# The opening of a two-layer trunk with its column blocks dealt out anew and one narrow block for the gates, and another order of retention's items

## The chip, the cores and the metric

The kernel runs on one core of one Trainium2 chip. The metric is the time of the whole program on the device, in microseconds (us). Five engines matter in what follows: PE (TensorE, the matrix unit; PEld is its loading of the stationary operand), DVE (VectorE), ACT (ScalarE), POOL (GpSimd) and SP (SyncE, which here only issues transfers). Each works through its own list of instructions; between engines there are semaphores.

## The reference

A vector `c` is turned into a modulation vector, and a trunk of two layers works on `x` of 1024 positions by 1024 features. Layer 0 mixes with a gated delta rule (GDN), layer 1 with retention; a gated feed-forward part with a short causal convolution follows each.

```python
e = silu(c @ cond_w + cond_b)                      # 1024 x 1024
for i in range(2):
    sh1, sc1, g1, sh2, sc2, g2 = split(e @ ada_w[i] + ada_b[i], 6)   # 1024 x 6144
    y = mixers[i](x * (1.0 + sc1) + sh1)
    x = layer_norm(DN_ALPHA * x + (1.0 + g1) * y, ln_g[i, 0], ln_b[i, 0])
    y = conv_ffn(x * (1.0 + sc2) + sh2, ...)
    x = layer_norm(DN_ALPHA * x + (1.0 + g2) * y, ln_g[i, 1], ln_b[i, 1])

def gated_deltanet(h, w_in, ...):                  # 8 heads of 128, chunks of 64
    qkv, z, a, bt = split(h @ w_in, [3072, 4096, 4104])   # a and bt: 8 columns each
    qkv = silu(causal_dwconv(qkv, conv_w))         # 4 taps
    beta = sigmoid(bt);  g = -exp(a_log) * softplus(a + dt_bias)
    ...                                            # triangular solve and a scan over chunks

def retention(h, w_in, w_out):                     # 4 heads, 256 wide keys, 512 wide values
    q, k, v, gate = split(h @ w_in, [1024, 2048, 4096])
    q, k = rot(q), rot(k)                          # rotary positions
    ...                                            # decayed attention in chunks of 128
    o = standardize(o) * silu(gate)
    return o @ w_out
```

`a` and `bt` together are the 16 columns called the gates' columns of GDN here. Retention's `gate` (2048 columns) is something else.

## The kernel before, in words

All arrays are float32. A product that has to be exact is made of three matmuls in the fast float32 form: each operand is split into a high part (a rounding copy on ACT, line 89) and a low part (a subtraction on DVE, line 90), and PE adds up high by low, low by high and high by high (`mm3`, lines 107 to 112). A tile is 128 partitions wide; rows of x are handled in two halves of 512. A load of a weight block of 1024 x 128 is one transfer of 512 KB (`load_w`, line 102).

**Opening.** `cond_w` arrives in 8 pieces of 128 rows (line 182, two halves of 256 KB each). Of the 1024 output columns DVE takes 512, multiplying and adding piece by piece into `mva` (lines 184 and 186); PE takes the other four blocks of 128 columns, one accumulation bank each (`by_cols`, line 175). `col_sum` (line 170) then sums DVE's part over the partitions by four small matmuls with a vector of ones. With the bias and Silu this is `e` (line 203). The first quarter of the first layer's modulation (`mod_cols(0)`, lines 539 to 551) goes the same way, with 256 columns on DVE and two blocks on PE; quarters 1 to 3 are all DVE's, 512 columns each, with a column sum on PE (line 546). Their results are the scale and shift of features 2g and 2g+1 of h.

Four blocks of GDN's input weights are worked on meanwhile (`load_first`): block 0 is `wab`, the 16 gates' columns filled up with zeros to 128, blocks 1 to 3 belong to q, k and v. `x` is transposed on PE (`turn`, line 560, the copy at line 571). `first_k(half, f)` scales one feature block of 128 (line 577), splits it into `hT` (lines 89, 90) and adds its products into the accumulators: four for half 0, two for half 1. Between pairs of features stands one quarter of the modulation, so the opening has four stages. In the trace, line 110 is high by low, line 111 low by high, line 112 high by high. At the end the gates' columns are copied off (`ab`, line 634), transposed on PE (line 670) and worked into `g` and `beta` (lines 742, 743).

**Retention's input product.** The 3072 columns of q, k and gate are made with Strassen's scheme (`strassen`): for each item seven products (line 1179 in the trace) and sums on DVE and ACT. The list `mixed` says in which order the items come. A rope item applies the rotary positions with six DVE operations per half (lines 1672 to 1677), reading tiles with sines and cosines, and stores its halves to `qd` from ACT's queue (line 1679). A gate item applies Silu (line 1688) and stores to `gd` (line 1689). Both use the tiles called `pc`. After the last item the 2048 columns of v follow as an ordinary product (line 667), whose weights `ret_wv` are loaded at line 102 into the two-tile pool `wr`; half 1 of h comes back in pieces `xlo` (line 1705), turned at line 280. Meanwhile the residual is scaled by the layer norm's gain (`xg`, loads at lines 399 and 403, POOL at lines 409 and 410, stores at line 411), and q and k are read back (line 1843).

**What sets the order.** Within GDN's and retention's cores PE's order comes from a planner in the file; elsewhere the code's order is rearranged when the program is built, by a scheduler that times the engines by estimates. All loads and some stores are issued by SP in one order, and a load whose target is not yet free holds up every load behind it; the stores of `qd` and `gd` are issued by ACT. Tiles come from small pools (`wr` 2, `hTa` 8, `aux` 4, `auh` 8, `t2` 3), accumulators from 4 + 2 + 2 PSUM banks (`acc`, `mm`, `sc`).

## Time and profile before

| | us |
|---|---|
| median of three runs | 2954.41 (2944.8, 2956.14, 2954.41) |
| the profiled execution's own time | 2954.0 |
| its span, first to last instruction | 2952.2 |
| PE busy | 2822.2 (96%) |
| DVE busy | 2212.5 (75%) |
| ACT busy | 1316.4 (45%) |
| POOL busy | 494.4 (17%) |
| mean granted clock of TensorE | 0.982 |

PE's busy time is that of its records, whose ends are modelled; a chain of matmuls that starts one every 0.227 us counts as fully busy. The profile gives, for any stretch of time, the busy time of each engine with its number of instructions, the clock, the share of the transfer engines' time and their rate, and a timeline with what each instruction had waited for. Two stretches are of interest below: the opening, 0 to about 90 us, and the change from retention's items to its v product, about 1735 to 1770 us.

### The profile page before, as it was taken

The page shows a single profiled execution, that of the slowest core. Times are in us where ns is not written, and L with a number is a line of the kernel's source. Part 1 is how long each engine was busy: PE and PEld are TensorE (multiplying, and loading weights), DVE is VectorE, ACT ScalarE, POOL GpSimd, SP SyncE. Part 2 cuts the span into 40 slices and gives each one's busy share as a digit, 9 for nine tenths or more (in the row PEclk, how much of TensorE's full clock was granted, in tenths as well). Part 3 has the DMA queues.
Part 4 walks back from the last instruction along what each step waited for, and adds up shares of the span by engine and source line. Part 5 has one row for each costly group of instructions (what it writes and reads, how often), then busy time and mean ns, then how long its engine had stood idle before and what let it go on. Part 6 is the DMA issues. An engine that isn't in the chain of part 4 may idle for free.

```text
span 2952.2 us, 38981 instructions
## 1 busy us (share of the span) xinstructions
PE 2822.2 (96%) x13638; PEld 2306.3 (78%) x13638; DVE 2212.5 (75%) x3973; ACT 1316.4 (45%) x2413; POOL 494.4 (17%) x517
## 2 busy tenths in 40 slices
PE   8999898999999999998999999999999899999997
PEld 7787777887787888887878877777777788888886
DVE  5788787656688888958686665666779787777779
ACT  4745565444544444545333332221344544445543
POOL 0312221100013332000000012422202023331001
PEclk9999999999999999999999999999999999999999
DMA  7232222253255655855343364655673353334853
GB/s 277 86 108 68 83 79 80 83 166 138 93 178 173 213 187 191 300 156 176 130 140 121 115 217 154 210 170 164 186 242 125 106 168 128 136 129 161 293 182 114
DMA packets 248276, 459.40 MB, mean 156 GB/s; under 512 B 23632, under 2 KB 77136, under 8 KB 248080
## 3 DMA queue, kind: packets, MB, share of 16 engines
q1 hardware_dynamic: 215680, 405.27, 41.8%
q10 hardware_dynamic: 29760, 43.00, 4.0%
q0 software_dynamic: 2640, 8.65, 0.8%
q8 instruction: 107, 1.75, 0.3%
q14 instruction: 89, 0.73, 0.1%
HBM read 344.11 MB, written 112.72 MB: 155 GB/s over the span
## 4 chain that ended last, share of the span: by engine, by line
PE 73%; DVE 13%; DMA 6%; ACT 4%; issue 2%; POOL 1%; SPq 0%; POOLq 0%; ACTq 0%; DVEq 0%
PE acc L667 15%; PE acc L1179 9%; PE acc L110 5%; PE acc L111 5%; PE acc L112 5%; PE sc L1179 4%; PE sc L667 4%; PE acc L1454 3%; PE mm L667 3%; PE sc L111 2%; PE sc L112 2%; PE sc L110 2%; DVE o L1583 1%; PE mm L1454 1%; PE sc L1454 1%
## 5 line engine op out<-in xcount | busy, mean ns | idle before, releaser
L667 PE MATMUL acc<-hT,wh 128*128 128x512 f32 x960 | 300.2, 394 | 0.0
L1454 PE MATMUL acc<-bb,ab 128*128 128x512 f32 x984 | 236.7, 399 | 12.1 <-DVE bb L90 10.5
L1454 PEld LDWEIGHTS acc<-bb,ab 128*128 128x128 f32 x984 | 186.4, 191 | 56.1 <-DVE bb L90 15.5
L1179 PE MATMUL acc<-T,wb 128*128 128x512 f32 x840 | 203.2, 391 | 6.3 <-DVE wb L90 6.2
L667 PEld LDWEIGHTS acc<-hT,wh 128*128 128x128 f32 x960 | 182.3, 190 | 34.1
L89 ACT ACTIVATE ab<-ar 128x512 fp32r<-128x512 f32 x210 | 130.1, 626 | 166.5 <-PE mm L301 47.8
L667 PE MATMUL acc<-hT,wl 128*128 128x512 f32 x480 | 201.3, 419 | 0.0
L90 DVE TENSOR_TENSOR ab<-ar,ab 128x512 fp32r<-128x512 f32 x210 | 148.5, 713 | 65.2 <-ACT ab L89 65.2
L409 POOL TENSOR_TENSOR xg<-xg,gb 128x512 f32<-128x512 f32 x48 | 62.6, 1304 | 776.3 <-DMA xg<-xs 453.1
L1179 PEld LDWEIGHTS acc<-T,wb 128*128 128x128 f32 x840 | 156.7, 188 | 43.6 <-DVE wb L90 9.0
L90 DVE TENSOR_TENSOR wl<-wr,wh 128x1024 fp32r<-128x1024 f32 x95 | 119.8, 1262 | 88.3 <-ACT wh L89 88.1
L90 DVE TENSOR_TENSOR wb<-wr,wb 128x512 fp32r<-128x512 f32 x162 | 115.8, 720 | 71.5 <-ACT wb L89 71.4
L89 ACT ACTIVATE wh<-wr 128x1024 fp32r<-128x1024 f32 x95 | 100.7, 1061 | 146.4 <-PE acc L667 66.9
L90 DVE TENSOR_TENSOR wb<-mm,wb 128x512 fp32r<-128x512 f32 x216 | 145.8, 684 | 26.5 <-ACT wb L89 25.7
L1604 POOL TENSOR_TENSOR o<-o 128x512 f32<-128x512 f32 x80 | 111.7, 1405 | 287.6 <-ACT pc L1240 190.0
L1583 DVE SCALAR_TENSOR_TENSOR o<-g,vc,o 128x512 f32<-128x512 f32 (+2 forms) x176 | 154.7, 896 | 5.3 <-ACT o L1578 4.7
L89 ACT ACTIVATE wb<-mm 128x512 fp32r<-128x512 f32 x216 | 124.1, 595 | 59.8 <-DVE mm L1229 55.0
L1240 ACT ACTIVATE pc<-acc 128x512 f32<-128x512 f32 x143 | 84.8, 593 | 145.3 <-PE acc L1179 93.1
L89 ACT ACTIVATE wb<-wr 128x512 fp32r<-128x512 f32 x162 | 98.4, 627 | 104.5 <-DMA wr<-in_ffn_up 49.3
L667 PE MATMUL acc<-wh,hT 128*128 128x512 f32 x384 | 139.2, 425 | 2.9 <-DVE vv L90 1.7
L110 PE MATMUL acc<-T,wb 128*128 128x512 f32 x292 | 116.0, 397 | 9.4 <-DVE wb L90 9.4
L488 DVE SCALAR_TENSOR_TENSOR qkv<-raw,vc,qkv 128x512 f32<-128x512 f32 x144 | 111.7, 780 | 11.5 <-ACT qkv L486 10.7
(639 smaller groups left out, 7488.1 us busy)
## 6 DMA issues: line engine op xcount, KB each, us to landing
wr<-in_ffn_up SPq DMA_DIRECT2D x92, 512.0 KB, 4.3
mvw<-in_ada_w SPq DMA_DIRECT2D x80, 512.0 KB, 4.5
ad<-o SPq DMA_DIRECT2D x154, 256.0 KB, 3.1
ar<-ad SPq DMA_DIRECT2D x154, 256.0 KB, 3.8
Br<-in_ffn_down SPq DMA_DIRECT2D x88, 256.0 KB, 3.4
wr<-in_ret_wv SPq DMA_DIRECT2D x32, 512.0 KB, 4.1
ar<-od SPq DMA_DIRECT2D x56, 256.0 KB, 5.3
xs<-xt ACTq DMA_DIRECT2D x24, 512.0 KB, 3.8
```

What stands on the lines that cost most here:

```text
L89: act.activation(dst_h, src, AF.Copy)
L90: eng.tensor_tensor(dst_l, src, dst_h, ALU.subtract)
L110: mm(acc, wl[:, k], hl[0], start=first, stop=False)
L111: mm(acc, wh[:, k], hl[1], start=False, stop=False)
L112: mm(acc, wh[:, k], hl[0], start=False, stop=last)
L488: dve.scalar_tensor_tensor(oh, raw[:, 3 - j:515 - j], w[:, 3 - j:4 - j], oh, ALU.mult, ALU.add)
L667: pq(pe.matmul(out, lhsT, rhs, start=start, stop=stop), cost)
L1179: return pe.matmul(*a, skip_group_check=True, **kw)
L1240: act.activation(t, X, AF.Copy)
L1454: return pe.matmul(*args, skip_group_check=True, **kw)
L1583: dve.scalar_tensor_tensor(tv, gv[:, c0 - j:c1 - j], w[:, 2 - j:3 - j], tv, ALU.mult, ALU.add)
L1604: (dve if fp == 0 else pool).tensor_tensor(o[d], o[x], o[y], op)
```

## The change

1. **cond_w.** DVE takes five of the eight column blocks of `cond_w` (640 columns), PE three. The sum over the partitions covers five blocks.
2. **First quarter of the modulation.** DVE takes three blocks (384 columns), PE one.
3. **The gates' columns.** `wab` is laid out as 128 rows of 8 x 32 values, the 16 columns twice for each of the 8 feature blocks (128 KB instead of 512 KB). On the chip the second 16 of each 32 are replaced by their low part. A product with the gates' columns then takes two matmuls with 32 output rows (the high and low weight columns against `hT` high, and against `hT` low) instead of three with 128. The low part's rows are added after the transposes in `gates()`, by a copy and an addition per half; the copies and transposes cover 32 partitions instead of 128. A matmul with 32 stationary columns is in PE's form of 128 x 32 tiles, not 128 x 128.
4. **First stage.** The loads of the four weight blocks are issued together, and the splits, the turns and the products of features 0 and 1 are written block by block.
5. **Retention's items.** After two gate items the order was r r g r g r g r r g r g r g (r a rope item, g a gate item); it is now r r g r g r r g r g r r g g.

```diff
-    def col_sum(a, tile=None):
-        pt = (tile or mm_tile)()
-        for j in range(4 * len(a)):
-            pe.matmul(pt[:, j:j + 1], a[j // 4][:, j % 4 * P:j % 4 * P + P], ones[:, 0:1], start=True, stop=True)
+    def col_sum(a, n, tile):
+        pt = tile()
+        for j in range(n):
+            pe.matmul(pt[:, j:j + 1], a[:, j * P:(j + 1) * P], ones[:, 0:1], start=True, stop=True)
         return pt
 
     def by_cols(banks, w, v, k):
         for j, bank in enumerate(banks):
             pe.matmul(bank[:, 0:1], w[:, j * P:(j + 1) * P], v[:, k:k + 1], start=(k == 0), stop=(k == KT - 1))
 
-    a0 = tl("t2", [P, HALF], name="mva")
-    cbank = acc4()
+    NV = 5
+    a0 = tl("wr", [P, NV * P], name="mva")
+    cbank = [acc_tile() for _ in range(KT - NV)]
     for k in range(KT):
-        w = two("hTa", F32, "mvw")
+        w = tl("hTa", [P, D], name="mvw")
         for hf in range(2):
-            sp.dma_start(w[hf], A["cond_w"][k * P:(k + 1) * P, hs(hf)])
+            sp.dma_start(w[:, hs(hf)], A["cond_w"][k * P:(k + 1) * P, hs(hf)])
+        wv = w[:, 0:NV * P]
         if k == 0:
-            dve.tensor_scalar(a0, w[0], cT[:, 0:1], None, ALU.mult)
+            dve.tensor_scalar(a0, wv, cT[:, 0:1], None, ALU.mult)
         else:
-            dve.scalar_tensor_tensor(a0, w[0], cT[:, k:k + 1], a0, ALU.mult, ALU.add)
-        by_cols(cbank, w[1], cT, k)
+            dve.scalar_tensor_tensor(a0, wv, cT[:, k:k + 1], a0, ALU.mult, ALU.add)
+        by_cols(cbank, w[:, NV * P:], cT, k)
...
-    pt = col_sum([a0])
+    pt = col_sum(a0, NV, mm_tile)
...
+    raw1 = []
+    AB = 4 * GH
+
     def load_first(n):
         ti = first[n]
-        src = A["gdn_wab"] if ti is None else A["gdn_wqkv"][ti]
-        ws.append(load_w(src, ("wh", "wl") if n < 2 else ("aux", "aux"), "hTa"))
+        raw1.append(tl("hTa", [P, KT * AB if ti is None else D], name="wr"))
+        sp.dma_start(raw1[n], A["gdn_wab"] if ti is None else A["gdn_wqkv"][ti])
+
+    def split_first(n):
+        if first[n] is None:
+            w = tl("wh", [P, KT * AB], F32R, name="wab")
+            act.activation(w, raw1[n], AF.Copy)
+            wv, rv = [t.rearrange("p (k n) -> p k n", n=AB) for t in (w, raw1[n])]
+            dve.tensor_tensor(wv[:, :, AB // 2:], rv[:, :, AB // 2:], wv[:, :, AB // 2:], ALU.subtract)
+            ws.append(wv)
+            return
+        tags = ("wh", "wl") if n == 1 else ("aux", "aux")
+        w = [tl(tags[0], [P, D], F32R, name="wh"), tl(tags[1], [P, D], F32R, name="wl")]
+        split(w[0], w[1], raw1[n])
+        ws.append((kn(w[0]), kn(w[1])))
...
-    def mod_cols(g):
+    def mod_mul(g):
         w = mw[g]
-        n = 2 * P if g == 0 else HALF
+        n = 3 * P if g == 0 else HALF
         a = tl("t2", [P, HALF], name="mva")[:, 0:n]
-        bank = [sc_tile(), sc_tile()] if g == 0 else None
+        bank = sc_tile() if g == 0 else None
         for k in range(KT):
             wk = w[k // 2][:, k % 2] if g < 2 else w[k]
             if k == 0:
@@ -540,17 +558,23 @@
             else:
                 dve.scalar_tensor_tensor(a, wk[:, 0:n], e[:, k:k + 1], a, ALU.mult, ALU.add)
             if g == 0:
-                by_cols(bank, wk[:, n:], e, k)
-        pt = mm_tile()
-        for j in range(n // P):
-            pe.matmul(pt[:, j:j + 1], a[:, j * P:(j + 1) * P], ones[:, 0:1], start=True, stop=True)
-        c = slice(2 * g, 2 * g + 2)
+                by_cols([bank], wk[:, n:], e, k)
+        return a, bank
+
+    def mod_sum(g, a, bank):
+        c0 = 2 * g
+        c = slice(c0, c0 + 2)
+        if g == 0:
+            pt = col_sum(a, 3, sc_tile)
+            dve.tensor_add(sh1[:, 1:2], bank[:, 0:1], bias_cols(0, 0)[:, 1:2])
+            dve.tensor_add(sh1[:, 0:1], pt[:, 2:3], bias_cols(0, 0)[:, 0:1])
+        else:
+            pt = col_sum(a, 4, mm_tile)
+            dve.tensor_add(sh1[:, c], pt[:, 2:4], bias_cols(0, 0)[:, c])
         dve.scalar_tensor_tensor(sc1[:, c], pt[:, 0:2], 1.0, bias_cols(0, 1)[:, c], ALU.add, ALU.add)
-        if g == 0:
-            for j in range(2):
-                dve.tensor_add(sh1[:, j:j + 1], bank[j][:, 0:1], bias_cols(0, 0)[:, j:j + 1])
-        else:
-            dve.tensor_add(sh1[:, c], pt[:, 2:4], bias_cols(0, 0)[:, c])
+
+    def mod_cols(g):
+        mod_sum(g, *mod_mul(g))
...
-    def first_k(half, f):
+    def first_h(half, f):
         src = xT[half, f] if (half, f) in xT else turn(half, f)
         tmp = tl("t2", [P, HALF])
         act.activation(tmp, src, AF.Identity, bias=sh1[:, f:f + 1], scale=sc1[:, f:f + 1])
         ht = two(("hTa", "hTb")[half], F32R, "hT")
         split(ht[0], ht[1], tmp)
         hT[half].append(ht)
+
+    def first_mm(half, f, n):
         if accs[half] is None:
             accs[half] = [sc_tile(), sc_tile()] if half else acc4()
-        for n, acc in enumerate(accs[half]):
-            mm3(acc, ws[n], f, ht, f == 0, f == KT - 1)
+        acc, ht, last = accs[half][n], hT[half][f], f == KT - 1
+        if n:
+            mm3(acc, ws[n], f, ht, f == 0, last)
+        else:
+            pe.matmul(acc[0:AB], ws[0][:, f], ht[0], start=(f == 0), stop=False)
+            pe.matmul(acc[0:AB], ws[0][:, f], ht[1], start=False, stop=last)
+
+    def first_k(half, f):
+        first_h(half, f)
+        for n in range(2 if half else 4):
+            first_mm(half, f, n)
...
     load_x(0, 0)
-    load_first(0)
-    mod_cols(0)
-    hold(0, range(2, 4))
-    for n in range(1, 4):
+    for n in range(4):
         load_first(n)
     mod_loads(1)
     load_x(0, 1)
-    first_k(0, 0)
-    first_k(0, 1)
+    m0 = mod_mul(0)
+    split_first(0)
+    hold(0, range(2, 4))
+    for f in range(2):
+        xT[0, f] = turn(0, f)
+    mod_sum(0, *m0)
+    for f in range(2):
+        first_h(0, f)
+        split_first(1 + f)
+        for k in range(f + 1):
+            first_mm(0, k, 1 + f)
+        if f:
+            first_mm(0, 1, 1)
+        first_mm(0, f, 0)
+    split_first(3)
+    for f in range(2):
+        first_mm(0, f, 3)
...
-            act.activation(t[:, 0:HALF], acc, AF.Copy)
+            act.activation(t[0:AB, 0:HALF], acc[0:AB], AF.Copy)
...
-                ptr(pt[:, c * P:(c + 1) * P], abh[q4][:, c * P:(c + 1) * P])
+                pq(pe.transpose(pt[:, c * P:c * P + AB], abh[q4][0:AB, c * P:(c + 1) * P], ident[0:AB, 0:AB]), 0.109)
             pv = v4(pt)
             cs = slice(q4 * 4, (q4 + 1) * 4)
-            dve.tensor_tensor(g64[:, cs], pv[:, :, 0:GH], bm(dtb, 4), ALU.add)
-            dve.tensor_copy(beta[:, cs], pv[:, :, GH:2 * GH])
+            ab = tl("sm2", [P, 4, 2 * GH], name="ab")
+            dve.tensor_copy(ab, pv[:, :, 0:2 * GH])
+            dve.tensor_tensor(ab, pv[:, :, 2 * GH:4 * GH], ab, ALU.add)
+            dve.tensor_tensor(g64[:, cs], ab[:, :, 0:GH], bm(dtb, 4), ALU.add)
+            dve.tensor_copy(beta[:, cs], ab[:, :, GH:2 * GH])
...
-    mixed = [ropes.pop(0)] + [r for k in range(3) for r in (ropes.pop(0), gates_.pop(0))] + [ropes.pop(0)]
-    mixed += [r for k in range(3) for r in (ropes.pop(0), gates_.pop(0))]
+    mixed = [(ropes if q == "r" else gates_).pop(0) for q in "rrgrgrrgrgrrgg"]
...
-    wab = np.zeros((D, P), w.dtype)
-    wab[:, 0:16] = w[:, 4096:4112]
-    o["gdn_wab"] = _units(wab)[0]
+    wab = np.concatenate([w[:, 4096:4112]] * 2, axis=1)
+    o["gdn_wab"] = wab.reshape(KT, P, 4 * GH).transpose(1, 0, 2).reshape(P, KT * 4 * GH)
```

What this does to the instruction lists is shown at three places. In the first, ACT before `hT` exists: the stretch from `e` to the first two split features, before.

```order
L203 ACTIVATE e<-e 128x8
L89 ACTIVATE wh<-hTa 128x1024 x3
L571 ACTIVATE xT<-mm 128x512 x2
L89 ACTIVATE wh<-hTa 128x1024
L577 ACTIVATE t_278<-mm,v_173,v_172 128x512
L577 ACTIVATE t_304<-mm,v_173,v_172 128x512
L89 ACTIVATE hT<-t_278 128x512
L89 ACTIVATE hT<-t_304 128x512
```

The same stretch of ACT after; `wab` is the narrow block, `wr` there are the raw weights.

```order
L205 ACTIVATE e<-e 128x8
L534 ACTIVATE wab<-wr 128x256
L595 ACTIVATE xT<-mm 128x512 x2
L89 ACTIVATE wh<-wr 128x1024
L601 ACTIVATE t_253<-mm,v_164,v_163 128x512
L89 ACTIVATE wh<-wr 128x1024
L601 ACTIVATE t_271<-mm,v_164,v_163 128x512
L89 ACTIVATE hT<-t_253 128x512
L89 ACTIVATE wh<-wr 128x1024
L89 ACTIVATE hT<-t_271 128x512
```

The three wide weight splits now stand among the scaling and splitting of the features instead of ahead of them. The second place is PE at the start of the second stage, the column sum of quarter 1, the turns and the first products, before.

```order
L546 MATMUL mm<-ones,mva 128x1 x4
L560 MATMUL mm<-cst,xt 128x128 x16
L110 MATMUL acc<-hT,wl 128x512 x4
L111 MATMUL acc<-hT,wh 128x512
L112 MATMUL acc<-hT,wh 128x512
```

And after, where matmuls into 32 rows stand singly between those into 128.

```order
L170 MATMUL mm<-ones,mva 128x1 x4
L584 MATMUL mm<-cst,xt 128x128 x16
L613 MATMUL acc<-hT,wab 32x512
L110 MATMUL acc<-hT,wl 128x512 x3
L614 MATMUL acc<-hT,wab 32x512
L111 MATMUL acc<-hT,wh 128x512
L112 MATMUL acc<-hT,wh 128x512
```

One of four L110 and one of four pairs L111, L112 are gone for two single matmuls, so that PE goes from the wide form to the narrow one and back twice per feature. The third place is SP where the last items of retention's input product end and the v product begins, before.

```order
L403 DMA xg<-xs_67 128x512
L1843 DMA qk<-qd 128x512 x2
L399 DMA gb<-in_ln_g 128x512
L411 DMA xg_169<-xg 128x512
L399 DMA gb<-in_ln_b 128x512
L403 DMA xg<-xs_67 128x512 x2
L1843 DMA qk<-qd 128x512 x2
L102 DMA wr<-in_ret_wv 128x1024
L1705 DMA xlo<-xs_67 128x512
L102 DMA wr<-in_ret_wv 128x1024
L411 DMA xg_169<-xg 128x512
L1705 DMA xlo<-xs_67 128x512
```

And after (`L1892` is what was L1843, `L1754` what was L1705, `L405` and `L413` what were L403 and L411).

```order
L405 DMA xg<-xs_67 128x512 x3
L1285 DMA wr<-in_ret_wg 128x1024
L1286 DMA wr<-in_ret_wg 128x1024
L413 DMA xg_160<-xg 128x512 x3
L405 DMA xg<-xs_67 128x512 x2
L413 DMA xg_160<-xg 128x512
L102 DMA wr<-in_ret_wv 128x1024
L413 DMA xg_160<-xg 128x512
L1892 DMA qk<-qd 128x512 x3
L102 DMA wr<-in_ret_wv 128x1024
L1892 DMA qk<-qd 128x512
L1754 DMA xlo<-xs_67 128x512 x2
```

Of the three pairs of reads of q and k (`qk`) that stood 12, 6 and 1 rows ahead of the first `ret_wv`, the last is gone from there; in the new list two pairs stand 14 and 10 rows ahead of it (above the rows shown). The second pair, and with it loads and stores of `xg`, now also stand ahead of the last gate item's weights (L1285, L1286), which before stood just ahead of the rows shown.

More of the change, by code (lines that the diff above doesn't have):

```diff
@@ L196, in vcol @@
         return vc[:, a:a + n]
-    pt = col_sum([a0])
+    pt = col_sum(a0, NV, mm_tile)
     e = ct("e", [P, KT])
-    for j in range(4):
-        dve.tensor_add(e[:, 4 + j:5 + j], cbank[j][:, 0:1], vcol("cond_b")[:, 4 + j:5 + j])
-    dve.tensor_add(e[:, 0:4], pt[:, 0:4], vcol("cond_b")[:, 0:4])
+    for j, bank in enumerate(cbank):
+        dve.tensor_add(e[:, NV + j:NV + 1 + j], bank[:, 0:1], vcol("cond_b")[:, NV + j:NV + 1 + j])
+    dve.tensor_add(e[:, 0:NV], pt[:, 0:NV], vcol("cond_b")[:, 0:NV])
     act.activation(e, e, AF.Silu)
```

## Prediction

> **What bounds the kernel.** I read the page's busy times and chain first, to see which engine a gain must come from, then windows over the two stretches that the change touches, then their timelines. The page's first part and the head of its chain:
>
> ```profile
> PE 2822.2 (96%) x13638; PEld 2306.3 (78%) x13638; DVE 2212.5 (75%) x3973; ACT 1316.4 (45%) x2413; POOL 494.4 (17%) x517
> PE 73%; DVE 13%; DMA 6%; ACT 4%; issue 2%; POOL 1%; SPq 0%; POOLq 0%; ACTq 0%; DVEq 0%
> ```
>
> PE is the bound nearly everywhere: only 4% of the span are without it. A change of two short stretches can win the idle time of those stretches, or take matmuls away, and no more. The opening by windows (time; then busy us with instruction counts of PE, PEld, DVE, ACT, POOL; granted clock; transfer share; GB/s):
>
> ```profile
> 0.00:50.00 50.00, 39.06 (x185) 35.47 (x186) 28.12 (x51) 15.48 (x23) 1.13 (x11) 1.00 0.96 354
> 50.00:100.00 50.00, 46.36 (x221) 37.57 (x220) 31.32 (x57) 34.03 (x53) 5.67 (x6) 0.97 0.29 91
> 100.00:200.00 100.00, 100.00 (x471) 83.29 (x470) 88.40 (x200) 60.05 (x120) 24.69 (x40) 1.00 0.30 96
> ```
>
> In the first 50 us PE idles 11 us and the transfer engines are full; in the next 50 it idles 3.6 us; after 100 us it never does.
>
> The opening's timeline (start, duration, engine, what; in brackets the idle time before and what ended it):
>
> ```profile
> 6.85 14.03 PE L175 MATMUL acc<-cT,mvw 128*128 128x1 f32 x64 [6.85 <-DMA mvw<-in_cond_w]
> 20.74 1.84 PE L170 MATMUL mm<-ones,mva 128*128 128x1 f32 x8
> 23.08 6.99 PE L175 MATMUL sc<-e,mvw 128*128 128x1 f32 x32 [0.49 <-ACT e L203]
> 29.93 0.99 PE L546 MATMUL mm<-ones,mva 128*128 128x1 f32 x4
> 30.78 3.75 PE L560 MATMUL mm<-cst,xt 128*128 128x128 f32 x16
> 36.22 1.20 PE L110 MATMUL acc<-hT,wl 128*128 128x512 f32 x4 [1.68 <-ACT hT L89]
> 39.37 1.08 PE L110 MATMUL acc<-hT,wl 128*128 128x512 f32 x4
> 40.28 0.39 PE L111 MATMUL acc<-hT,wh 128*128 128x512 f32 x1
> 42.70 1.02 PE L546 MATMUL mm<-ones,mva 128*128 128x1 f32 x8 [0.45 <-DVE mva L541]
> 14.93 0.75 DVE L186 SCALAR_TENSOR_TENSOR mva<-mvw,cT,mva 128x512 f32<-128x512 f32 x1 [0.60 <-DMA mvw<-in_cond_w]
> 16.28 0.75 DVE L186 SCALAR_TENSOR_TENSOR mva<-mvw,cT,mva 128x512 f32<-128x512 f32 x1 [0.60 <-DMA mvw<-in_cond_w]
> 23.45 3.61 DVE L541 SCALAR_TENSOR_TENSOR mva<-mvw,e,mva 128x256 f32<-128x256 f32 x7
> 31.04 2.36 DVE L90 TENSOR_TENSOR wl<-hTa,wh 128x1024 fp32r<-128x1024 f32 x2
> 37.87 4.68 DVE L541 SCALAR_TENSOR_TENSOR mva<-mvw,e,mva 128x512 f32<-128x512 f32 x6
> 33.26 1.05 ACT L89 ACTIVATE wh<-hTa 128x1024 fp32r<-128x1024 f32 x1
> 34.21 1.44 ACT L577 ACTIVATE t<-mm,v,v 128x512 f32<-128x512 f32 x2
> 35.53 1.15 ACT L89 ACTIVATE hT<-t 128x512 fp32r<-128x512 f32 x2
> ```
>
> One fp32 matrix-by-vector instruction leaves two records, 0.219 us each (14.03 / 64). A matmul of 512 columns starts every 0.227 us ((40.28 − 39.37) / 4).
>
> **The change, part by part.**
>
> *The gates' sums.* `gates()` has two more small DVE operations per half, run after 100 us where PE never waits: nothing. If that cover went, 4 operations of at most 0.52 us (that of 256 columns above, 3.61 / 7) would be 2 us.
>
> *cond_w.* PE is late here, not the transfers: the last half lands about 16.95 (the pieces come 1.35 us apart, 14.93 and 16.28, each in two halves), and PE ends at 20.88. With 48 records instead of 64 it needs 10.5 us, so it is held by the last half: 16.95 + 6 × 0.219 = 18.3. DVE's operation grows from 512 to 640 columns: 0.75 us at 512 and 0.52 at 256 give 0.87, done at 17.8, hidden by PE. The column sum has 10 records of 0.23: 20.6. From its end (22.58) to PE's next start (23.08) it took 0.5 us: `e` is used at 21.1 instead of 23.08, **−2.0**.
>
> *First quarter of the modulation.* DVE: one operation and seven of 384 columns (0.52 + 0.12 = 0.63): 4.9 us, done at 26.0; PE's 16 records take 3.5 us and are hidden. The column sum (6 records, 1.5 us) ends at 27.5, the scale is there at 28.0; before, at about 31.1 (the L546 row ends at 30.92, and a short DVE operation follows). So **−3.1** at this point.
>
> *The narrow block's load* is 384 KB less, 1.1 us at the first window's 354 GB/s, for every load behind it. I cost it at nothing, since the ACT list below, not the loads, is what comes last; it would give at most that 1.1.
>
> *From there to the first product* ACT sets the pace. The turns stand behind the column sum on PE, so the first is done near 27.8. Then ACT has two copies (0.72 each, like the scalings, 1.44 / 2), and now the weight splits of 1.05 that were ahead of it before: split, scaling, split, scaling, `hT` (0.58): 27.8 + 1.44 + 2 × 1.05 + 1.44 + 0.58 = 33.4 for PE's first product, which started at 36.22. Another split and `hT` make it 35.0 for the second feature. DVE has by then a `wl` of 1.2 (from 34.45 on), a low part of 0.6 and seven operations of quarter 1, one more than the six of the row of 4.68 since one less fits in ahead: 36.3 + 4.68 + 0.75 = 41.75, against 42.55 before. What was 3.1 earlier is **−0.8** where stage 2 starts (both ends: −3.1 if DVE takes quarter 1 ahead of the splits, 0 if one more weight block is late). The two narrow matmuls per feature lie in that slack, in which PE waits some 2 us more than before.
>
> *Stages 2 to 4* I take as PE's, as the second window has it (46.36 of 50). For features 2 to 7 of half 0 and all 8 of half 1, 14 times, one matmul of three goes: −14 × 0.227 = **−3.2**. Against it stands the change of form. The narrow matmul is of the form 128 x 32 and stands alone between wide ones; the two of one feature are neighbours once, so there are 27 excursions. The trace has no excursion of this form. The nearest rows are those where GDN's 32 x 32 matmuls stand in a stream of wide ones, and the mean of one (203 ns):
>
> ```profile
> 219.95 0.62 PE L667 MATMUL acc<-hT,wh 128*128 128x512 f32 x2
> 220.50 2.11 PE L667 MATMUL mm<-T,U 32*32 32x32 f32 x64
> 222.54 0.50 PE L667 MATMUL acc<-hT,wl 128*128 128x512 f32 x1
> 222.87 0.63 PE L667 MATMUL acc<-hT,wh 128*128 128x512 f32 x2
> L667 PE MATMUL mm<-T,U 32*32 32x32 f32 x256 | 9.7, 203 | 2.1 <-DVE qkv L944 2.1
> ```
>
> The two wide ones would let the next start at 219.95 + 0.454 = 220.40; it starts at 220.50, +0.10. The small ones start 0.030 apart ((2.11 − 0.20) / 63), the last at 222.41, and the wide one at 222.54 rather than 222.44, +0.10. The one after it comes 0.33 later instead of 0.227, +0.10. I take 0.29 per excursion, 27 × 0.29 = **+7.8**. Lower end 0: the loss may belong to the many small matmuls. Upper end 0.55: the wide record grows to 0.50 at the switch, and if nothing overlaps on either side an excursion costs 2 × (0.50 − 0.227). I stay at the row, which is the same engine in the same stream. [...]
>
> *The end of the opening.*
>
> ```profile
> 79.74 0.66 PE L670 MATMUL mm<-cst,ab 128*128 128x128 f32 x4 [0.65 <-ACT t L577]
> 80.93 0.73 PE L110 MATMUL sc<-hT,wl 128*128 128x512 f32 x2 [0.53 <-ACT hT L89]
> 82.52 0.70 PE L111 MATMUL sc<-hT,wh 128*128 128x512 f32 x1 [0.86 <-DVE hT L90]
> 83.00:86.00 3.00, 3.00 (x8) 2.34 (x7) 0.07 (x1) 0.00 (x0) 0.00 (x0) 0.50 0.02 5
> ```
>
> PE idles 2.0 us waiting for a late split of half 1, and then runs at half clock for 3 us, where 8 matmuls cost 3.0 us instead of 1.8. A PE that is 0.29 slower per excursion is waited for more and waits less. I take **−2.0**, between 0 and −3.2.
>
> *Retention's end.* The waits of SP and PE, and the timeline:
>
> ```profile
> SPq L1843 <- DVE rm L1672: 11.7, 2, 10.9
> SPq L102 <- DMA qd<-pc: 4.0, 1, 4.0
> 1752.42 3.02 PE L1179 MATMUL sc<-T,wb 128*128 128x512 f32 x12
> 1750.55 0.33 SPq L102 DMA_DIRECT2D wr<-in_ret_wv  x1
> 1757.91 1.06 ACT L89 ACTIVATE wh<-wr 128x1024 fp32r<-128x1024 f32 x1 [4.28 <-DMA xlo<-xs]
> 1746.38 0.68 DVE L90 TENSOR_TENSOR wb<-wr,wb 128x512 fp32r<-128x512 f32 x1
> 1758.80:1765.60 6.80, 6.12 (x14) 4.51 (x15) 4.26 (x4) 2.83 (x5) 3.43 (x2) 0.51 1.03 386
> ```
>
> SP's reads of q wait 10.9 us for the last rope item to be done with its tiles, and the first load of `ret_wv` waits 4.0 us for a store of `qd`. It goes out at 1750.55 and its split starts at 1757.91, 7.4 later. PE has ended the items at 1755.4 (1752.42 + 3.02), has next to nothing until 1758.8 (3 us lost), and then does 14 matmuls in 6.8 us at half clock (3.2 us of work, 3.6 lost): 6.6 us. With two gates last, the tiles for the rope are done with an item earlier and no `qd` store is near. The raw block's last reader is over at 1747.1, so the load can go at about 1747.1, be split from 1754.5 on if it takes 7.4 again, and PE gets the high part as the items end and the low part 1 us later: **−5**, between 0 (loads and stores of `xg` now stand ahead of it on SP, and they wait for POOL) and −6.6.
>
> *The items' order elsewhere.* What follows a rope item costs PE idle time, more when it is another rope item:
>
> ```profile
> 1520.00:1530.00 10.00, 8.94 (x40) 7.09 (x39) 9.74 (x17) 4.04 (x8) 0.00 (x0) 1.00 0.15 57
> 1700.00:1710.00 10.00, 9.39 (x41) 7.46 (x41) 8.77 (x15) 4.04 (x7) 0.00 (x0) 1.00 0.79 219
> ```
>
> The first is rope after rope (1.06 idle), the second a rope item's successor of the other kind (0.61). The new order has three pairs of ropes instead of two: **+0.45**. Moved weight loads: the last gate item's weights now stand on SP behind a pair of reads of q and k; those wait for the last rope, which is an item earlier, and I cost that at nothing as long as they arrive some 4 us ahead of their use; without that cover it is a wait of a few us on PE.
>
> Sum: −0.8 − 3.2 + 7.8 − 2.0 − 5 + 0.45 = −2.8. From the profiled execution's 2954.0 (0.4 below the median of 2954.41): **2951**.
>
> **The rivals.** *B, the switch costs nothing*: for it speaks that no narrow matmul of 512 columns is in the trace, against it the three gaps of 0.10. Without the 7.8 the sum is −10.6: **2943**. *C, retention's end stays as it is*, because `ret_wv` waits behind the stores of `xg`, whose scaling on POOL comes late: for it speaks that SP holds a list in order and waited 10.9 us for one row of it; against, that POOL is busy 17%. Without the 5: **2956**. [...]
>
> **How the numbers follow.** The forecast has 0.50, B 0.18, C 0.13, D 0.13; 0.06 is for what I don't see, of either sign. The forecast's own terms reach from −7 to +3 of its 2951. The range takes in B with its bounds (2940) and D with the same (2962). About 0.5% (14.8 us) is what a measurement of this kernel can tell from no change; that is below 2939.6 or above 2969. Only B with every bound in its favour, or the unseen, goes below: 0.08. D with retention's gain gone too, or a stall that I don't see, goes above: 0.07. Within: 0.85.
>
> **What would show it.** Right: `e` used near 21 us; the first wide product near 33.4; the second stage's column sum near 41.8; around each single narrow matmul a gap of some 0.3 us between wide ones; the opening as a whole one or two us longer at 100 us; `ret_wv` issued near 1747 of the old time and no stretch of half clock behind the last item. Wrong: narrow matmuls that start 0.227 after their neighbour (B); a wait of PE for the wide weights at the items' end (C), or within the last gate item; gaps of 0.5 (D); a new stretch of half clock in the 2 us that PE waits ahead of stage 2.

## The result, and the profile after

The changed kernel takes 2941.57 us (median of 20 runs, 2937.3 to 2949.42), the kernel before, run beside it, 2950.57 us (20 runs, 2942.52 to 2958.44). The medians lie 9.0 us apart; the ratio of the runs is 0.9976, 95% interval 0.9967 to 0.9984: 7 us faster, between 5 and 10. The forecast was 3 us faster, with a range of 2940 to 2962.

The page of the changed kernel has this for its engines.

```profile
span 2942.7 us, 38900 instructions
PE 2815.8 (96%) x13594; PEld 2298.3 (78%) x13594; DVE 2208.4 (75%) x3976; ACT 1314.9 (45%) x2413; POOL 497.8 (17%) x517
```

PE's share is what it was; its busy time is 6.4 us less. To see where the time went, I paired equal PE instructions of two traces and took the difference of their times. Relative to the first trace of the kernel before, with a second trace of each kernel, this stands at some points of the old time (us, negative is earlier):

| point of the old time | before, again | changed | changed, again |
|---|---|---|---|
| 100 | -1.2 | -6.6 | -4.6 |
| 545 | -1.4 | -3.9 | -2.6 |
| 600 | -1.4 | -0.2 | +1.1 |
| 1700 | -1.2 | -1.8 | +2.0 |
| 1750 | -1.2 | +0.1 | +3.7 |
| 1900 | -1.4 | -6.3 | -3.0 |
| end of the span | -5.0 | -9.5 | -4.3 |

The two second traces are of single runs of 2949.0 us (before) and 2949.74 us (changed).

Three places stand out in both traces of the change: the opening wins 4.6 to 6.6, the stretch from 545 to 600 loses 3.7, and retention's end, from 1700 to 1900, wins 4.5 to 5.0, net of a loss of 1.7 to 1.9 up to 1750. What lies between drifts by a few us in every trace, the kernel before against itself included.

*The opening.* By windows, as before:

```profile
0.00:50.00 50.00, 37.28 (x156) 31.98 (x157) 30.18 (x51) 14.49 (x23) 1.13 (x11) 0.97 0.97 356
50.00:100.00 50.00, 47.49 (x238) 37.13 (x237) 35.09 (x65) 35.59 (x57) 4.99 (x7) 1.00 0.30 98
```

The clock of 0.97 in the first window is a piece of half clock of 3.41 us, from 44.6; in the second trace of the changed kernel pieces fell at 42.5 (6.83 us) and 56.2 (3.41 us). Two kernels below with the same narrow block and no half clock ahead of 78 us are 7.0 ahead at 100 us, so the difference between 4.6 and 6.6 goes with these pieces.

And PE's timeline in the first stage, with the narrow products (L613, L614) and the second column sum (the L170 row at 40.89):

```profile
21.02 3.58 PE L175 MATMUL sc<-e,mvw 128*128 128x1 f32 x16 [0.50 <-ACT e L205]
32.73 0.80 PE L110 MATMUL acc<-hT,wl 128*128 128x512 f32 x1 [2.26 <-ACT hT L89]
33.32 0.63 PE L613 MATMUL acc<-hT,wab 128*32 128x512 f32 x1
33.75 0.63 PE L110 MATMUL acc<-hT,wl 128*128 128x512 f32 x1
...
39.33 0.39 PE L112 MATMUL acc<-hT,wh 128*128 128x512 f32 x1
39.55 0.40 PE L614 MATMUL acc<-hT,wab 128*32 128x512 f32 x1
39.79 0.39 PE L111 MATMUL acc<-hT,wh 128*128 128x512 f32 x1
40.02 0.39 PE L112 MATMUL acc<-hT,wh 128*128 128x512 f32 x1
40.89 1.02 PE L170 MATMUL mm<-ones,mva 128*128 128x1 f32 x8 [0.49 <-DVE mva L559]
```

The narrow matmul at 39.55 starts 0.22 after the wide one ahead of it, the wide one behind it 0.24 later, and the next 0.23 after that. There is no gap: a change to the form of 128 x 32 and back costs 0.01 us (three starts in 0.69 us instead of 3 x 0.227 = 0.68; 0.01 is also the median of 15 such excursions of this trace), not 0.29. At the end of the opening, where PE idled 2.0 us and then ran at half clock, only this is left:

```profile
79.21 0.42 PE L614 MATMUL sc<-hT,wab 128*32 128x512 f32 x1 [0.91 <-DVE hT L90]
80.30 0.43 PE L786 MATMUL mm<-cst,ab 32*128 32x32 f32 x4 [0.21 <-ACT ab L681]
```

*545 to 600 us*, in a stretch of GDN whose code the change does not touch. PE's longest wait there, of the kernel before and then of the changed one:

```profile
PE acc L670 <- ACT qkv L489: 3.3, 1, 3.3
```

```profile
PE mm L714 <- DVE qkv L994: 4.2, 1, 4.2
562.00:572.00 10.00, 7.89 (x30) 6.84 (x31) 4.82 (x8) 3.83 (x20) 0.00 (x0) 0.66 0.07 26
```

The wait is 0.9 longer and is followed by a stretch of half clock that the kernel before did not have. The build order moved. On DVE, three operations of the convolution and a weight split stand between the last steps of the last of GDN's triangular inverses, where before they came ahead of them or after. DVE's list there before, from the inverse's last two steps on (fs and T are the inverse, RX its transpose, qkv with L488 the convolution):

```
L833 fs<-Y,T 128x31    L835 T<-T,fs 128x31    L838 RX<-T
L488 qkv<-raw,vc,qkv   L90 wl<-wr,wh          L842 TX<-TP
```

and after:

```
L885 T<-T,fs 128x87    L490 qkv<-raw,vc,qkv   L883 fs<-Y,T 128x60   L90 wl<-wr,wh
L490 qkv<-raw,vc,qkv   L885 T<-T,fs 128x60    L490 qkv<-raw,vc,qkv  L883 fs<-Y,T 128x31
L885 T<-T,fs 128x31    L888 RX<-T
```

The transpose at its end, before and after:

```profile
550.13 1.25 DVE L838 STREAM_TRANSPOSE RX<-T 128x1024 f32<-128x1024 f32 x1
```

```profile
550.48 1.25 DVE L888 STREAM_TRANSPOSE RX<-T 128x1024 f32<-128x1024 f32 x1
```

PE is 3.9 us ahead of the old trace here, and the transpose is 0.35 behind it. From there both kernels go through ACT's copies of the inverse (L869 before, L919 after). What stands between these copies and the end of PE's wait, before and after:

```profile
557.86 3.92 ACT L869 ACTIVATE T<-TX 32x256 f32<-32x256 f32 x6 [0.40 <-ACT sg L1104]
561.81 0.63 ACT L489 ACTIVATE qkv<-qkv 128x512 f32<-128x512 f32 x1
```

```profile
556.98 3.98 ACT L919 ACTIVATE T<-TX 32x256 f32<-32x256 f32 x6
563.29 0.17 DVE L511 TENSOR_SCALAR ssq<-ssq 128x8 f32<-128x8 f32 x1 [4.62 <-ACT sq L509]
563.38 0.68 DVE L994 TENSOR_TENSOR qkv<-mm,ir 128x512 f32<-128x512 f32 x1
```

Before, the `qkv` that PE waits for is ACT's next operation after the copies. In the changed kernel ACT first makes eight squares (L509), DVE's step on their sums (L511) waits for these, and the `qkv` that PE waits for (L994) stands behind that step in DVE's list. So the order of DVE and ACT together makes the wait, not the inverse's lateness on DVE alone. In each of the seven traces with this order the same rows end the wait.

*Retention's end.* PE's waits between 1715 and 1775 us in the changed kernel, and the rows that answer to those shown of before:

```profile
PE acc L1229 <- DVE wb L90: 1.3, 2, 1.1
PE sc L110 <- DVE wb L90: 0.6, 1, 0.6
PE mm L282 <- DMA xlo<-xs: 0.4, 1, 0.4
```

```profile
1726.73 0.33 SPq L1285 DMA_DIRECT2D wr<-in_ret_wg  x1
1734.60 1.15 ACT L89 ACTIVATE wb<-wr 128x512 fp32r<-128x512 f32 x2 [0.96 <-DMA wr<-in_ret_wg]
1736.01 0.50 PE L110 MATMUL sc<-hT,wb 128*128 128x512 f32 x1 [0.57 <-DVE wb L90]
1744.56 0.33 SPq L102 DMA_DIRECT2D wr<-in_ret_wv  x1
1748.69 1.06 ACT L89 ACTIVATE wh<-wr 128x1024 fp32r<-128x1024 f32 x1 [0.87 <-DMA wr<-in_ret_wv]
1754.96 0.39 PE L112 MATMUL sc<-T,wb 128*128 128x512 f32 x1
1755.18 0.39 PE L714 MATMUL acc<-wh,hT 128*128 128x512 f32 x1
```

`ret_wv` goes out 6.0 us earlier than before, is split 9.2 earlier, and the v product (L714) follows the last item's product without a gap. Ahead of this PE waits 1.9 us in the two last gate items (2.0 in the second trace). 1.06 of it stand in the first of them, which follows two rope items, with 0.25 more later in that item (none in the second trace). The last 0.57 (0.87) are where the last gate item begins: its first weight load, which stands behind the reads of q and k and loads of `xg` on SP, went out at 1726.73 and took 7.8 us to land (3.4 in the kernel before), so that its split began at 1734.60.

### The profile page after: what moved, and what is told of

Same layout as the page of the kernel before. It is cut to its first block, busy times and chain, and to the rows that moved or that the text cites. A ratio compares the mean times of both kernels' runs of the same rounds, so it can differ in the third digit from the quotient of the medians.

```text
span 2942.7 us, 38900 instructions
## 1 busy us (share of the span) xinstructions
PE 2815.8 (96%) x13594; PEld 2298.3 (78%) x13594; DVE 2208.4 (75%) x3976; ACT 1314.9 (45%) x2413; POOL 497.8 (17%) x517
## 5 line engine op out<-in xcount | busy, mean ns | idle before, releaser
L714 PE MATMUL acc<-hT,wh 128*128 128x512 f32 x960 | 301.3, 395 | 0.0
L714 PEld LDWEIGHTS acc<-hT,wh 128*128 128x128 f32 x960 | 183.4, 191 | 34.5
L714 PE MATMUL acc<-hT,wl 128*128 128x512 f32 x480 | 202.3, 421 | 0.0
L411 POOL TENSOR_TENSOR xg<-xg,gb 128x512 f32<-128x512 f32 x48 | 62.4, 1302 | 773.6 <-DMA xg<-xs 761.4
L1654 POOL TENSOR_TENSOR o<-o 128x512 f32<-128x512 f32 x80 | 124.7, 1568 | 288.8 <-ACT pc L1290 190.1
L714 PE MATMUL acc<-wh,hT 128*128 128x512 f32 x384 | 135.2, 416 | 1.0 <-DVE vv L90 1.0
L110 PE MATMUL acc<-T,wb 128*128 128x512 f32 x292 | 116.0, 397 | 9.4 <-DVE wb L90 9.4
```

The source lines that it names most:

```text
L110: mm(acc, wl[:, k], hl[0], start=first, stop=False)
L714: pq(pe.matmul(out, lhsT, rhs, start=start, stop=stop), cost)
L1654: (dve if fp == 0 else pool).tensor_tensor(o[d], o[x], o[y], op)
```

## The experiments

**The traces once more.** The unchanged file of the kernel before, and that of the changed kernel, each profiled again.

> The kernel before, profiled once more. In the two traces at hand the changed kernel is 6.6 us ahead at 100 us, only 0.2 us ahead at 600 us, 1.4 us ahead at 1650 us and 8.0 us ahead at 1800 us. Theory 'chance': the 6.4 us given back between 100 and 600 us is where stretches of half clock happen to fall, and the same kernel's own second trace differs from its first by 3 us or more there. Theory 'order': it belongs to the changed kernel, and the two traces of the kernel before agree within 1.5 us in that stretch.

> The changed kernel, profiled once more. Theory 'chance': its stretch from 100 to 600 us differs by 3 us or more from its first trace. Theory 'order': it agrees within 1.5 us and PE again waits some 4 us at about 560 us for DVE. Both: the opening at 100 us and the end of retention's items agree with the first trace within 1 us.

The numbers are in the table above: between 545 and 600 us the kernel before differs from itself by 0.0, the changed kernel loses 3.7 both times, and the wait of 3.2 or 4.1 us recurs.

```profile
PE acc L670 <- ACT qkv L489: 3.2, 1, 3.2
```

```profile
PE mm L714 <- DVE qkv L994: 4.1, 1, 4.1
```

The first line is the kernel before, the second the changed one. At this place it is order, not chance. The opening agreed less well than I said (6.6 and 4.6; in the second trace half clock fell twice into it, 6.8 us from 43 and 3.4 from 56), and elsewhere the traces differ by some us: 200 to 400 us lose 3.2 and 2.5 in the two of the change, while five of the kernels below whose lists on PE, DVE and ACT are the same there win 0.3 to 2.5, so that is chance.

**The two halves of the change.** The kernel before with the new order of items alone, and the changed kernel with the old one.

```diff
-    mixed = [ropes.pop(0)] + [r for k in range(3) for r in (ropes.pop(0), gates_.pop(0))] + [ropes.pop(0)]
-    mixed += [r for k in range(3) for r in (ropes.pop(0), gates_.pop(0))]
+    mixed = [(ropes if q == "r" else gates_).pop(0) for q in "rrgrgrrgrgrrgg"]
```

> The kernel before with only retention's items in the new order. Theory: the v product starts without the two waits and without half clock, so that the stretch from 1700 to 1800 us is 6 us shorter (8 won at the end, 2 lost in the last items), ratio about 0.998. Rival: the gain needs the earlier opening or the rest of the change, and the time is that of the kernel before within 2 us.

> The changed kernel with the items in the old order. Theory: 6.6 us ahead at 100 us as in the full change; if what is given back up to 600 us is chance, the time is 5 to 7 us under the kernel before (ratio 0.998); if it is the new order of GDN's instructions, it is within 2 us of the kernel before (ratio 0.9995 to 1). The wait of 7 us at the end of retention's items is back in both.

Items alone: 2944.79 us against 2950.99, ratio 0.9982 (0.9971 to 0.9992). From 1700 to 1900 us it wins 4.3, without the rest of the change. Opening alone: 2951.71 us, ratio 1.0000 (0.9991 to 1.0008), though it is 7.0 us ahead at 100 us; 2.3 of these are lost again from 545 to 600 us, after the same wait of 4.1 us. The items carry the measured gain; of the opening's gain the interval leaves at most 3 us at the end.

**The loss at 560 us: which part makes it.** The changed kernel with `cond_w` dealt out as before, and the kernel before with `cond_w` alone dealt out anew.

```diff
-    NV = 5
+    NV = 4
```

> The changed kernel with cond_w dealt out as before, four column blocks on DVE and four on PE; everything else as changed. In this build the scheduler leaves GDN's last triangular inverse on DVE as in the kernel before. Theory 'order': between 545 and 600 us it loses less than 0.5 us against the kernel before (the changed kernel lost 3.7 in both traces), the opening gains 1 to 2 us less than the changed kernel's 4.6 to 6.6, and the time is 1 to 3 us under the changed kernel's, ratio 0.9965 to 0.997. Theory 'chance': it loses 2 to 4 us there all the same, and the time is 2 us over the changed kernel's.

> The kernel before with cond_w alone dealt out anew (five blocks on DVE, three on PE). In this build the scheduler orders GDN's last triangular inverse as in the changed kernel, though nothing of the gates' block or of the items is changed. Theory 'order': e is used 2.0 us earlier, but 545 to 600 us loses 2.3 to 3.7 us, and the time is that of the kernel before or up to 2 us over it (ratio 1.000 to 1.0007). Theory 'the narrow block': no loss between 545 and 600 us, ratio 0.9993 to 1.

DVE's list at the last inverse is that of before in the first and the changed one in the second. PE's wait in the first, then in the second:

```profile
PE acc L717 <- ACT qkv L491: 3.2, 1, 3.2
```

```profile
PE mm L669 <- DVE qkv L946: 4.1, 1, 4.1
568.00:574.00 6.00, 5.06 (x18) 4.59 (x19) 2.91 (x6) 1.93 (x11) 0.00 (x0) 0.53 0.00 0
```

Between 545 and 600 us the first loses 0.0, the second 3.7. In the seven traces of this study with the changed order this stretch loses 2.2 or 2.3 us where one piece of half clock of 3.41 us followed the wait, and 3.7 where two did; in the other six with the old order it loses nothing but in one (1.5 us, with a piece of half clock). The second kernel here holds none of the gates' block and none of the items: the order is a side effect of the build. Not every shift of the opening tips it: `cond_w` and the first quarter dealt out anew together (below) leave the old order. As for time, the second is 2954.74 us, ratio 1.0007 (0.9995 to 1.0019), as expected. The first is 2944.81, ratio 0.9979 (0.9967 to 0.9990), and not the 0.9965 to 0.9970 expected: it was 8.4 us ahead at 600 us and 11.4 at 1900, but 8.8 at 2900. The place and its order are settled; that avoiding it makes the whole faster is not shown.

**The opening's parts.** The kernel before with `cond_w` and the first quarter dealt out anew and nothing else, and the kernel before with the narrow block alone.

```diff
+    NV = 5
...
+        n = 3 * P if g == 0 else HALF
```

```diff
+            pe.matmul(acc[0:AB], ws[0][:, f], ht[0], start=(f == 0), stop=False)
+            pe.matmul(acc[0:AB], ws[0][:, f], ht[1], start=False, stop=last)
```

> The kernel before with cond_w and the first quarter of the modulation dealt out as in the change, nothing else. Theory: the scale of the first features comes 3 us earlier, but the three weight splits on ACT and the wide loads still come first, so that the second stage starts less than 1.5 us earlier and 100 us is reached at most 2 us earlier. Rival: most of the opening's 5 us are due to this dealing, and 100 us is reached 4 us earlier or more.

> The kernel before with the gates' columns as one narrow block, in the old order of the first stage and with cond_w and the modulation as before. Theory: the 14 matmuls less in stages 2 to 4 (3.2 us) and the gates' waits and half clock at 80 to 86 us (up to 3.7 us) are this block's, so that 100 us is reached 3 to 6 us earlier than before; between 545 and 600 us 2 to 4 us are lost, since this build has GDN's last triangular inverse in the changed order. Rival: without the earlier first stage 100 us is reached at most 2 us earlier.

At 100 us the first is 0.1 behind the first trace of before (1.3 behind its second), the second 4.5 ahead. So most of the opening's gain belongs to the narrow block. The dealing of the columns was 1.3 ahead at the second stage's column sum, as reckoned, and lost it to a piece of half clock from 45.1; a piece from 46.4 cost the narrow block 1.1 as well. The new order of the first stage was not run by itself, so what it adds (the whole change is 4.6 to 7.0 ahead) stays open. The narrow block alone again has the wait of 4.1 us, and loses 2.2 there. Their single times are 2953.72 and 2951.28 us (before 2953.75).

**The change of form.** The changed kernel with the narrow block filled up to 128 stationary columns, and with the narrow products summed over 32 rows only.

```diff
-            pe.matmul(acc[0:AB], ws[0][:, f], ht[0], start=(f == 0), stop=False)
+            pe.matmul(acc, ws[0][:, f], ht[0], start=(f == 0), stop=False)
```

```diff
-            pe.matmul(acc[0:AB], ws[0][:, f], ht[0], start=(f == 0), stop=False)
+            pe.matmul(acc[0:AB], ws[0][0:32, f], ht[0][0:32], start=(f == 0), stop=False)
```

> The changed kernel with the gates' columns filled up with zeros on the chip to 128 stationary columns, so that its 32 products are in the wide form: no change of form, two matmuls instead of three as in the changed kernel. If a change of form costs 0.29 us as I had put it, the matmuls of stages 2 to 4 take 7.8 us less than in the changed kernel; if it costs nothing, neighbours start 0.23 us apart in both and the stretch from the first column sum to 100 us is the same within 1 us (apart from where half clock falls).

> The changed kernel with the gates' products summed over 32 of the 128 rows only, which leaves out three quarters of that sum: the same 32 single matmuls, now in the form of 32 x 32 tiles between wide ones. Theory 'rows': what costs time is a switch of the number of rows, as in the 32 x 32 stream of the first trace; each single excursion then costs 0.2 to 0.3 us, and the wide neighbour starts 0.4 to 0.5 us after the matmul ahead of the narrow one plus 0.227. Theory 'stream': the 0.3 belongs to the many small matmuls, and single ones cost 0 to 0.05 us in this form too.

In the first the column sum of stage 2 is at 40.72 (40.89 in the change), and at 100 us it is 4.6 ahead, as the change's second trace, which has its pieces of half clock at the same places (42.5 and 56.2). Its neighbours:

```profile
50.05 0.39 PE L616 MATMUL acc<-hT,wab 128*128 128x512 f32 x1
50.28 0.84 PE L110 MATMUL acc<-hT,wl 128*128 128x512 f32 x3
```

In the second, with 32 rows:

```profile
50.37 0.40 PE L112 MATMUL acc<-hT,wh 128*128 128x512 f32 x1
50.69 0.42 PE L613 MATMUL acc<-hT,wab 32*32 32x512 f32 x1
51.04 0.96 PE L110 MATMUL acc<-hT,wl 128*128 128x512 f32 x3
51.94 0.41 PE L614 MATMUL acc<-hT,wab 32*32 32x512 f32 x1
```

The narrow one starts 0.32 after its neighbour, the wide one 0.35 after that, and the three wide ones take 0.96 instead of 0.84: 0.09 + 0.12 + 0.12 = 0.33 per excursion (also the median of 12 of them), close to the 0.29 taken from the stream of 32 x 32 matmuls. At 100 us this kernel is 7.1 behind the kernel before, 11.7 to 13.7 behind the change; 27 x 0.33 = 8.9 of that are the excursions; of the rest, half clock has a part (two pieces of 6.83 us, from 69.9 and 90.3). Theory 'rows' holds against 'stream': a single 32 x 32 matmul between wide ones costs 0.33 us, a 128 x 32 one 0.01. A form with fewer rows and all columns was not run, so that the rows alone make the cost is not shown. The single times are 2948.38 and 2963.11 us (before 2951.33).

**What makes retention's end late.** The kernel before with a rope item last.

```diff
+    mixed = [(ropes if q == "r" else gates_).pop(0) for q in "rrgrgrgrgrgrgr"]
```

> The kernel before with another order of items, r r g r g r g r g r g r g r: the last item is a rope item, and the fewest rope items follow one another. In this build the pair of reads of q and k that waited 10.9 us stands behind the first load of ret_wv on SP, not ahead of it. Theory 'distance': the end is late since a rope item is close to it (its tiles, its stores of qd, its DVE work); the v product then starts later than in the kernel before, and the two waits for ret_wv and xlo and the half clock cost 7 us or more. Rival 'list': it is late since SP's list has reads ahead of ret_wv that wait for the rope; then ret_wv goes out about 1747 of the old time or sooner and the v product follows the items with less than 2 us of waits.

SP's rows, PE's only wait between 1715 and 1775 us, and PE at the items' end:

```profile
1743.24 0.33 SPq L102 DMA_DIRECT2D wr<-in_ret_wv  x1
1746.19 1.28 SPq L1842 DMA_DIRECT2D qk<-qd  x3
1748.51 0.38 SPq L1704 DMA_DIRECT2D xlo<-xs  x1
PE acc L1179 <- DVE wb L90: 0.6, 1, 0.6
1755.97 0.39 PE L112 MATMUL sc<-T,wb 128*128 128x512 f32 x1
1756.20 0.39 PE L667 MATMUL acc<-wh,hT 128*128 128x512 f32 x1
```

With the rope at the very end the v product follows without a gap. Rival 'list' holds: a rope item near the end does not by itself make the first `ret_wv` late; before, reads that waited for a rope item stood ahead of it on SP. The load's own wait of 4.0 us for a store of `qd` is gone here too, and how much of the lateness was that wait and how much the reads is not separated. From 1700 to 1900 us this order wins 7.0 (the change 4.5 to 5.0), has no wait in the last item, and the one run took 2944.37 us beside 2953.75. One run does not rank it.

**A third order.** The kernel with `cond_w` as before and everything else changed, with the third pair of rope items placed earlier.

```diff
-    mixed = [(ropes if q == "r" else gates_).pop(0) for q in "rrgrgrrgrgrrgg"]
+    mixed = [(ropes if q == "r" else gates_).pop(0) for q in "rrgrrgrrgrgrgg"]
```

> The kernel with cond_w dealt out as before and the rest as changed, and with the items in a third order, r r g r r g r r g r g r g g: two gates last as in the change, but the third pair of rope items lies earlier, so that the last rope item follows a gate item. Theory: the last gate item's second weight load waited for a store of qd of the last rope item; with DVE less behind there, PE's two waits in the last item (1.8 us in the run it is built on, 1.9 in the change) shrink to 1 us or less, and the time is 0 to 2 us under that kernel's 2944.8, ratio to before 0.997 to 0.998. Rival: the load waits for the last rope item wherever the pair lies, and the waits stay at 1.5 us or more.

```profile
PE sc L110 <- DVE wb L90: 1.7, 1, 1.7
PE acc L1229 <- DVE wb L90: 0.6, 1, 0.6
```

The waits stay, 2.3 us, and to that extent the rival holds, but they moved: the item behind the rope now waits 0.6 instead of 1.5, and the last item begins 1.7 late instead of 0.3. It is that item's first weight load, 7.7 us from issue to landing, and not the second as I had it, that PE waits for. The time is 2944.35 us (before 2953.75), ratio 0.9969 (0.9958 to 0.9981), the lowest ratio of these kernels; its interval overlaps that of the change (0.9967 to 0.9984), so it is not shown to be better.

## Why the prediction was right, and where it was not

The direction, the size within a factor of three and the range were right; the sum was off by 4 us, by one large term, one that was missing, and two at retention's end that offset each other. Part of this is luck. I had the opening lose 1.8 us (−0.8 − 3.2 + 7.8 − 2.0) and be longer at 100 us, where it is 4.6 to 6.6 ahead: the direction came from retention's end alone, and a cost of 7.8 that does not exist stood in part for a loss at 560 us that I had not seen.

- *cond_w and the first quarter.* Right: `e` was used at 21.02 (21.1 said), the scale was there at about 27.8 (28.0), the first product came at 32.73 (33.4), the second column sum at 40.89 (41.8). That most of the 2 us at `e` and 3 at the scale is lost by stage 2 was right too, as the dealing alone shows (1.3 ahead at the second column sum). A sign of being wrong came as well: new half clock at the start of stage 2 (from 44.6).
- *The price of a change of form*, +7.8: the step that failed. The row I took it from changes rows and columns at once, the change only columns. It is 0.01 per excursion, some 0.3 in all. That is rival B's mechanism, to which I had given 0.18. That its 2943 is within 1.5 us of the result is luck, since the kernel before took 2950.57 beside the change and not 2954.0; as a difference, B says −10.6 and the forecast −2.8, where −7 was measured. The upper end of the range, 2962, takes 0.55 per excursion (27 x 0.55 = 14.9 us, D): no run shows that term, and what the runs showed is 0.33 for 32 x 32 and 0.01 for 128 x 32, with the same 128 rows and fewer columns.
- *The matmuls saved and the end of the opening*, −3.2 and −2.0: about right. The narrow block alone was 4.5 ahead at 100 us. The waits at the end of the opening fell from 2.0 to 1.1 us.
- *What GDN's order costs* was missing from my sum: 2 to 4 us from 545 to 600 us. I had looked at the order only where the change's own terms stood, and took it that PE never waits after 100 us from a window that ends at 200; it waits 3.3 us at 560 already in the kernel before. That DVE's list differs at GDN's last inverse was there to be seen before any run.
- *Retention's end*, −5: the waits went but for 0.2 to 0.4 us for `xlo`, and the half clock with them (6.4 to 6.7 us from 1750 to 1900); the explanation was half wrong. I named the distance of the last rope item; it is what stands ahead of `ret_wv` in SP's list and what that waits for.
- *The items elsewhere*, +0.45: right, with a term missing beside it. Behind two rope items PE waits 1.06 us, behind one 0.61; from 1520 us on the kernel before has two and five of these waits, the changed one three and four. The last gate item's weight load, which I had costed at nothing while it arrives 4 us ahead of its use, landed 0.6 to 0.9 us ahead of it, and PE waits another 0.6 to 0.9 us for its split. The net at retention's end, from 1700 to 1900 us, is 4.5 to 5.0 (4.55 said).

By places the sum is then about −5 for the opening, +2 to +4 at 560 us and −4.5 to −5 for retention: −5.5 to −8, and −7 was measured. The medians confirm only retention's part (items alone, ratio 0.9982, some 5 us); the opening alone has a ratio of 1.0000, so that what its lead keeps after 560 us reaches the end is not shown.

## What to carry to other kernels

Price a change of PE's form by a row that changes the same thing: here single 32 x 32 matmuls cost 0.33 us per excursion and 128 x 32 ones 0.01. When a build's scheduler sets the order, compare the whole order of both builds, not only the edited places: dealing out `cond_w` anew, in the first 20 us, moved instructions half a millisecond later and gave back up to 3.7 us. Where the v product, or any next stage, waits for its first load, look at what stands ahead of that load in the issuing queue's list and what those entries wait for.

## What the runs showed of the hardware

*The clock after a wait.* Granted half clock comes in whole multiples of 3.41 us (3.41, 6.83 and so on to 17.07 in these traces; only the last piece of each trace, of 11.6 to 14.7 us, has another length). The wait at 560 us was 4.1 or 4.2 us in seven traces of this study, and half clock followed it in all seven; it was 3.2 or 3.3 us in seven others, and half clock followed in one of them. Without the last piece of each trace, half the summed length of the pieces is 32 to 48 us per execution, and it differs between traces of the same code (46.1 and 42.7 in the kernel before). That is one reason why effects of 2 to 3 us that every trace shows at their place are hard to find in the medians: of the last 13 runs of the kernel before, the shortest (2945.68 us) had a mean clock of 0.987, the longest (2959.72 us) 0.981.

*Half speed that the clock column does not show.* In the changed kernel the first wide matmuls start 0.43 us apart until 37.6 us, where they later start 0.23 apart, while the granted clock of that stretch is 1.00:

```profile
33.00:38.00 5.00, 5.00 (x13) 3.37 (x14) 4.93 (x8) 1.14 (x2) 0.00 (x0) 1.00 1.04 388
```

The starts 0.43 us apart are about half speed. The trace's record of the granted clock begins only at 37.82 us, and the column has 1.00 for the time ahead of it. In the kernel before the record begins at 34.87, ahead of the first wide matmul (36.22), which starts 0.23 us apart from its neighbours once they follow without a wait. In all 14 traces it begins between 33.5 and 42.6 us; wide matmuls that come sooner start 0.43 us apart, later ones 0.23. Small ones show it too: the column sums of the first stage start a record every 0.213 us, those of the second every 0.112 (8 records in 1.84 us at 20.74 and in 1.02 us at 42.70 in the kernel before). So, by these spacings, what PE did up to then ran at about half speed in both kernels, the 0.219 us per record that I reckoned with included, and full speed came 3 us later in the changed one's first trace. Here DVE was waited for afterwards (0.49 us ahead of the column sum), so it cost little.
